# A two-layer hybrid decoder trunk: weight splits, first norm, softmax blocks, score rows and section order changed

## The chip, the cores and the metric

The kernel runs on one core of a Trainium2 chip. The metric is device time of one execution in microseconds (us), as the median of the runs. The profile is one execution, taken by the hardware profiler. The engines are named as the profile names them: PE is TensorE's matmul and PEld its weight load, DVE is VectorE, ACT is ScalarE, POOL is GpSimd, SP is the engine that issues most of the DMAs. L143 is line 143 of the kernel before.

## The reference

A trunk of two layers over 512 tokens of width 1024, all in fp32. One layer is:

```
h = rms_norm(x, norm_mix); proj = h @ w_in                   # 1024 -> 2832 columns, three head groups
y_a = gated_delta_net(...)   # 4 heads of 64: causal conv of width 4, silu, l2-norm of q and k,
                             # triangular solves, a recurrent state, rms_norm, silu gate
y_b = mlstm(...)             # 4 heads of 64: exponential input gate, sigmoid forget gate, stabilised
y_c = sliding_window(...)    # 8 query heads, 2 key heads, window 128, sink logits, rotary on 16 of 64
x = x + concat(y_a, y_b, y_c) @ w_out
x = x + square(relu(rms_norm(x, norm_mlp) @ w_up)) @ w_down  # 1024 -> 4096 -> 1024
x = x + sigmoid(rms_norm(x, norm_ple) @ w_ple_gate) * (p @ w_ple_proj)
```

After the second layer there is a last `rms_norm`. The attention's softmax takes, for each query and head, the scores of the window and one sink logit: it subtracts the largest, exponentiates, and divides by the sum with the sink's term. The rotary angles are position times eight frequencies.

## The kernel before, in words

**Layout.** Activations lie feature-major: 8 tiles `X` of 128 features x 512 tokens. A projection's output tile of 128 columns is a sum of 8 products over the input tiles.

**Three products for each.** To keep fp32 accuracy at the rate of a reduced format, each operand is split into a rounded high part and the rest (`whi`, `wlo` for weights, `xsh`, `xsl` for activations), and `mm3` (L165 to L167) multiplies high x high, high x low and low x high into one PSUM tile. Almost all TensorE time is in these three lines.

**The weight stream.** Feature-major weights come as 404 chunks of four 128 x 128 tiles (`w_load_`, from L137): a 256 KB DMA on the SP queue into one of two `raw` buffers, a cast on ScalarE to `whi` (L141), and a subtraction to `wlo` (L143). For the first `WPOOL` = 272 tiles of a layer, which is 68 chunks, the subtraction runs on GpSimd, after that on VectorE. Two chunks are asked for ahead of use.

**The start.** The token-major projections (`tok`, L271 to L273) need 8 input tiles, loaded and split (L190, L191), and 8 chunks of weights, split on VectorE (L264). Meanwhile `Norm.add` squares the input tiles on ScalarE (L204) and sums them on GpSimd and VectorE (L205). `Norm.finish` then sums over features with matmuls against ones (L212), takes a reciprocal root in small VectorE steps on 128 x 4 (`rsqrt`, L172 to L181), and spreads it over the partitions with a matmul against the identity (`rb`, L220). All norms work so.

**The mixing part of a layer** is a list of sections, opened by `seg(name)`: gates and their cumulative sums (`gates`, `rows`, `cols`), six projections with the convolution (`conv`: L440 scales, L443 is the first of four taps, L445 the others, on a tile that starts with three zeroed columns, L439), the squared lengths of queries and keys (`pss`, L455, with 32 output rows a tile, turned by transposes at L461), the triangular systems and their inverses (`decay`, `binv`, `dbl`), the scan over blocks, the mLSTM (`mlproj`, `ml`: scores `psq`, L729 and L730), the rotary tables and products (`rope`), the attention (`swa`), the output gates (`og`) and the output projection in two groups (`out1`, `out2`). The second score product, L730, multiplies 64 rows of the key tile with the low part of the queries, `mql`; two heads share an `mql` tile. The tiles `mqh`, `mql` and the attention's outputs `ych`, `ycl` come from one tag of eight buffers (`yq`).

**The attention** works by units of one head pair and one block of 128 queries, with four units pending: scores to PSUM, a copy of the previous block (L823), a masked copy of the own block (L826), the maximum (L828), its combination with the sink (L830, L831), the exponentials with their sums (L834), the sink's term (L837, L838), the division (L839 to L841), two transposes, two masks (L852, L855) and the products with the values.

**What sets the order.** Each engine works its instructions in a fixed order. It is made when the kernel is built, by a planner that simulates the engines and takes, of the instructions that are ready, the one with the highest priority. The priority is the place in the program, shifted by `tc.high_priority(offset)`. Weight loads and a few others are shifted by `HPRI` = 200; each section of each layer by its entry in the table `PRI`. So the table moves whole sections against the stream of projections on all engines at once.

**The end.** The last three row tiles are worked by halves of 256 tokens; for each half the norm is formed and the eight tiles are multiplied by it (L1039) and written out (L1040). The first half's products run on GpSimd, the second's on VectorE but for two.

## Time and profile before

| | |
|---|---|
| median of 3 runs | 1397.26 us (1394.84 to 1398.58) |
| span of the profiled execution | 1397.6 us |
| the profiled execution's own time beside the span | the span itself is used; nothing is added around it |
| PE busy | 1352.9 us |
| DVE, ACT, POOL busy | 839.1, 599.4, 325.1 us |
| DMA, mean over the span | 93 GB/s |

The span runs from the first to the last instruction. A line of a group reads: line, engine, operation, tile written <- tiles read, size, count | busy us, mean ns of one | idle time of the engine before them and what ended it. A line of the waits reads: engine and what waited, <- what it waited for: us in total, times, longest. In a timeline a line starts with its start in us and its duration. PE's times are modelled: a matmul's duration is longer than the distance to the next one, since they are pipelined, so distances from start to start are used where the pace counts.

### The profile page before, as it was taken

The numbers are of one execution on the slowest core, as the hardware profiler recorded it, in microseconds if no ns is written. First come the engines' busy times: TensorE is split into PE (matmuls) and PEld (weight loads), VectorE is DVE, ScalarE is ACT, GpSimd is POOL, SyncE is SP. The second block draws the span as 40 slices with busy tenths as digits, with TensorE's granted clock in tenths as the row PEclk, the third lists the DMA queues.
The fourth block names the chain that finished last, engine by engine and source line by source line (L and its number), as shares of the span: only waits on it lengthen the run. The fifth ranks groups of instructions, "written<-read, shape, count | busy, mean of one in ns | idle before, by whom it ended". The sixth has DMA issues, their size and how long they took to land.

```text
span 1397.6 us, 20344 instructions
## 1 busy us (share of the span) xinstructions
PE 1352.9 (97%) x7334; PEld 1113.3 (80%) x7334; DVE 839.1 (60%) x1749; ACT 599.4 (43%) x1236; POOL 325.1 (23%) x302
## 2 busy tenths in 40 slices
PE   7999899999999999999999899999999999999996
PEld 7667788778888888888896678887888888888886
DVE  6877978674344444454758688886544434444555
ACT  5374354254243242443535545634433324234443
POOL 4443632362000000010235455326400000000112
PEclk9999989999999999999999999999999999999998
DMA  4333222233333333332433322212333333233332
GB/s 152 99 99 89 55 57 77 69 98 98 98 99 95 95 97 98 99 98 91 142 106 99 108 69 63 78 54 91 99 98 98 97 99 95 95 98 98 98 98 76
DMA packets 88596, 130.04 MB, mean 93 GB/s; under 512 B 21408, under 2 KB 30112, under 8 KB 88496
## 3 DMA queue, kind: packets, MB, share of 16 engines
q1 hardware_dynamic: 87408, 127.71, 30.0%
q8 instruction: 57, 0.93, 0.3%
q10 hardware_dynamic: 1088, 1.05, 0.2%
q14 instruction: 43, 0.35, 0.1%
HBM read 123.18 MB, written 5.54 MB: 92 GB/s over the span
## 4 chain that ended last, share of the span: by engine, by line
PE 80%; DVE 9%; ACT 3%; issue 3%; POOL 2%; DMA 1%; SPq 0%; DVEq 0%; POOLq 0%; ACTq 0%
PE down L166 8%; PE down L165 8%; PE down L167 8%; PE up L167 8%; PE up L165 8%; PE up L166 8%; PE proj L165 2%; PE proj L167 2%; PE proj L166 2%; PE gate L165 2%; PE gate L167 2%; PE gate L166 2%; PE outp L166 2%; PE outp L165 2%; PE outp L167 2%
## 5 line engine op out<-in xcount | busy, mean ns | idle before, releaser
L141 ACT ACTIVATE whi<-raw 128x512 fp32r<-128x512 f32 x404 | 253.3, 630 | 530.5 <-PE down L166 201.3
L143 DVE TENSOR_TENSOR wlo<-raw,whi 128x512 fp32r<-128x512 f32 x268 | 187.1, 700 | 132.9 <-ACT whi L141 132.6
L143 POOL TENSOR_TENSOR wlo<-raw,whi 128x512 fp32r<-128x512 f32 x136 | 185.2, 1364 | 203.8 <-ACT whi L141 191.9
L205 POOL TENSOR_TENSOR acc<-acc,sq 128x512 f32<-128x512 f32 x34 | 49.0, 1440 | 700.4 <-ACT sq L204 700.0
L167 PE MATMUL up<-xsh,wlo 128*128 128x512 f32 x512 | 199.4, 390 | 1.2 <-POOL wlo L143 1.2
L165 PE MATMUL up<-xsh,whi 128*128 128x512 f32 x512 | 199.6, 390 | 0.0
L166 PE MATMUL up<-xsl,whi 128*128 128x512 f32 x512 | 199.2, 389 | 0.0
L165 PE MATMUL down<-hidh,whi 128*128 128x512 f32 x512 | 199.2, 389 | 0.0
L166 PE MATMUL down<-hidl,whi 128*128 128x512 f32 x512 | 197.9, 389 | 0.0
L167 PE MATMUL down<-hidh,wlo 128*128 128x512 f32 x512 | 197.9, 389 | 0.0
L165 PE MATMUL proj<-xsh,whi 128*128 128x512 f32 x304 | 125.2, 412 | 9.0 <-DVE rdst L781 4.5
L167 PE MATMUL proj<-xsh,wlo 128*128 128x512 f32 x304 | 124.6, 410 | 5.3 <-POOL wlo L143 5.3
L166 PE MATMUL proj<-xsl,whi 128*128 128x512 f32 x304 | 123.4, 406 | 0.0
L167 PEld LDWEIGHTS up<-xsh,wlo 128*128 128x128 f32 x512 | 96.1, 188 | 22.7 <-POOL wlo L143 2.8
L165 PEld LDWEIGHTS down<-hidh,whi 128*128 128x128 f32 x512 | 96.1, 188 | 20.0
L167 PEld LDWEIGHTS down<-hidh,wlo 128*128 128x128 f32 x512 | 96.1, 188 | 20.0
L965 DVE TENSOR_TENSOR X<-X,down 128x512 f32<-128x512 f32 x64 | 44.0, 688 | 113.3 <-PE down L167 113.3
L165 PEld LDWEIGHTS up<-xsh,whi 128*128 128x128 f32 x512 | 96.1, 188 | 19.8
L166 PEld LDWEIGHTS down<-hidl,whi 128*128 128x128 f32 x512 | 96.1, 188 | 19.8
L166 PEld LDWEIGHTS up<-xsl,whi 128*128 128x128 f32 x512 | 96.1, 188 | 19.8
L956 DVE SCALAR_TENSOR_TENSOR ha<-up,R 128x512 f32<-128x512 f32 x64 | 44.1, 691 | 100.3 <-PE up L167 89.8
L165 PEld LDWEIGHTS proj<-xsh,whi 128*128 128x128 f32 x304 | 59.5, 196 | 25.2 <-DVE mql L689 4.3
(359 smaller groups left out, 2306.5 us busy)
## 6 DMA issues: line engine op xcount, KB each, us to landing
raw<-wfm SPq DMA_DIRECT2D x404, 256.0 KB, 2.6
X<-xT SPq DMA_DIRECT2D x16, 256.0 KB, 4.5
raw<-wtm SPq DMA_DIRECT2D x16, 200.0 KB, 2.4
gr<-scr SPq DMA_DIRECT2D x8, 256.0 KB, 4.4
Mr<-scr SPq DMA_DIRECT2D x8, 256.0 KB, 3.5
xd<-X SPq DMA_DIRECT2D x8, 256.0 KB, 2.0
X<-xd SPq DMA_DIRECT2D x8, 256.0 KB, 2.9
praw<-pT SPq DMA_DIRECT2D x2, 512.0 KB, 3.7
```

What stands on the lines that cost most here:

```text
L141: A.activation(out=hi, in_=raw, func=ACTF.Copy)
L143: (G if (i % NCH) * WC < WPOOL else V).tensor_tensor(lo, raw, f(hi), ALU.subtract)
L165: PE.matmul(out=ps, lhsT=wh, rhs=ah, start=start and k == 0, stop=False)
L166: PE.matmul(out=ps, lhsT=wh, rhs=al, start=False, stop=False)
L167: PE.matmul(out=ps, lhsT=wl, rhs=ah, start=False, stop=stop and k == n - 1)
L205: (G if self.n < 6 else V).tensor_tensor(self.acc, self.acc, q, ALU.add)
L956: V.scalar_tensor_tensor(a_t, ps, 0.0, R, ALU.max, ALU.mult)
L965: V.tensor_tensor(X[m], X[m], ps, ALU.add)
```

## The change

- `WPOOL` is 0: all weight splits of the stream run on VectorE. `HPRI` is 250.
- The first norm takes its sums of squares from a second copy of the input, token-major (`xK`, four loads of 512 KB), by ScalarE with an accumulated sum (`token_sums`). The sums on GpSimd and the matmuls against ones are not needed there.
- The rotary angles are computed by token on 128 x 4 x 8 elements (`rope_tables2`), spread into two tiles and turned by 8 transposes; this stands after the first norm, not ahead of the rotary products.
- The norm's row is spread by a transpose of a broadcast column (`row_of`), not by a matmul against the identity.
- The sums of squares of queries and keys are formed token-major, with the squares as weights and two columns of indicators: no copy and no transposes afterwards.
- The first tap of the convolution runs on ScalarE and is the one without a shift, so that no zeroed columns are needed.
- The mLSTM's low queries get a tile for each head, with the other half zeroed, and the second score product uses all 128 rows.
- The softmax works on two blocks at a time, with three such pairs pending.
- Copies in the inverses and two of the output gates' products go from VectorE to ScalarE; the DeltaNet's norm gain is applied later, with the factor 0.5.
- Small tiles are padded to multiples of 64 bytes (`pad`).
- One matmul of zeros is issued at the start.
- At the end, only the group of two tiles of the second half stays on GpSimd; all other products run on VectorE.
- The table of section priorities is a new one.

```diff
 PRI = {
-    ("tok", 0): -400, ("vb", 0): 100, ("scan", 0): 60, ("og", 0): -400, ("out1", 0): -400, ("ya", 0): 100,
-    ("gates", 1): -50, ("cols", 1): 100, ("binv", 1): -200, ("dbl", 1): -50, ("mlproj", 1): 200, ("ml", 1):
-    30, ("rope", 1): 60, ("og", 1): -200, ("out1", 1): -200, ("ya", 1): 30, ("out2", 1): 100,
+    ("tok", 0): -400, ("vb", 0): -100, ("scan", 0): -600, ("og", 0): 30, ("out1", 0): -400, ("ya", 0): -600,
+    ("nrmk", 0): -600, ("ml", 0): -100, ("conv", 0): 150, ("decay", 0): 30, ("mlproj", 0): -300,
+    ("out2", 0): -100, ("dbl", 0): 30, ("ycb", 0): -600, ("cols", 0): 150, ("gates", 0): -50, ("binv", 0): -300,
+    ("gates", 1): -300, ("cols", 1): -100, ("binv", 1): 100, ("dbl", 1): 600, ("mlproj", 1): 30, ("ml", 1): 30,
+    ("rope", 1): 200, ("og", 1): -100, ("out1", 1): -100, ("ya", 1): 400, ("out2", 1): 200, ("ycb", 1): -50,
+    ("mlfin", 1): 60, ("rows", 1): -600, ("tok", 1): 30, ("decay", 1): 30, ("swa", 1): -50,
 }
-WPOOL = 272
-HPRI = 200
+PEND2 = 3
+WPOOL = 0
+HPRI = 250
...
+def pad(pool, shape, tag, name, bufs, dt=F32):
+    n = int(np.prod(shape[1:]))
+    if n % 16 == 0:
+        return pool.tile(shape, dt, tag=tag, name=name, bufs=bufs)
+    t = pool.tile([shape[0], -(-n // 16) * 16], dt, tag=tag, name=name, bufs=bufs)[:, 0:n]
...
+    with tc.high_priority(offset=4000):
+        zt = tp.tile([128, T], F32, tag="acc", name="zt", bufs=1)
+        G.memset(zt, 0.0)
+        pw = ps_tile([128, T], "pw")
+        for _ in range(1):
+            PE.matmul(out=pw, lhsT=zt[:, 0:128], rhs=zt, start=True, stop=True)
...
+    def token_sums(raw):
+        ss = pad(tp, [128, NB], "sst", "sst", 1)
+        for b in range(NB):
+            x_b = raw([128, D], "xk")
+            nc.sync.dma_start(out=x_b, in_=xK[b])
+            A.activation(out=x_b, in_=x_b, func=ACTF.Square, accum_out=ss[:, b:b + 1])
+        return ss
+    def row_of(ps, v):
+        PE.transpose(ps, v.broadcast_to([128, 128]), ident)
...
+    def rope_tables2(us, small):
+        pi = small([128, NB], "pi").bitcast(I32)
+        nc.sync.dma_start(out=pi, in_=pos)
...
+        for j in range(2):
+            src = us([128, NB, 128], "rsrc")
+            G.memset(src, 1.0 - j)
+            src4 = src.rearrange("p b (h e f) -> p b h e f", h=2, f=8)
+            for h in range(2):
+                for e in range(2):
+                    V.tensor_scalar(src4[:, :, h, e, :], k[:, j], -1.0 if j and not e else 1.0, None, ALU.mult)
+            pt = mm_tile("prt")
+            for b in range(NB):
+                PE.transpose(pt[:, b * 128:(b + 1) * 128], src[:, b, :], ident)
+            tab = us([128, T], "rtab")
+            A.activation(out=tab, in_=pt, func=ACTF.Copy)
+            nc.sync.dma_start(out=rope_d[j], in_=tab)
...
-            raw = us([128, 3 + T], "craw")
-            G.memset(raw[:, 0:3], 0.0)
-            V.tensor_tensor(raw[:, 3:3 + T], ps, R, ALU.mult)
+            raw = us([128, T], "craw")
+            V.tensor_tensor(raw, ps, R, ALU.mult)
...
-            V.tensor_scalar(c_t, raw[:, 0:T], s_l[:, w0:w0 + 1], None, ALU.mult)
+            A.activation(out=c_t, in_=raw, func=ACTF.Copy, scale=s_l[:, w0 + 3:w0 + 4])
...
-                PE.matmul(out=pss[32 * i:32 * i + 32], lhsT=ind, rhs=sq, start=True, stop=True)
+                for b in range(NB):
+                    PE.matmul(out=pss[:, b, i, :], lhsT=sq[:, b * 128:(b + 1) * 128], rhs=ind[:, 0:2], start=True,
+                              stop=True)
...
+                        q_l = yq("mql")
+                        mql.append(q_l)
+                        G.memset(f(q_l[halves[1 - e]]), 0.0)
...
-                PE.matmul(out=psq[:, 128 * J:T], lhsT=mkS[h][hs, js], rhs=mql[h // 2][hs, 128 * J:T], start=False, stop=True)
+                hs = slice(0, 128)
+                PE.matmul(out=psq[:, 128 * J:T], lhsT=mkS[h][hs, js], rhs=mql[h][hs, 128 * J:T], start=False, stop=True)
...
-            mx = tt([128, 2], "smx", bufs=2)
+            mx = tt([128, 2, 2], "smx", bufs=2)
             V.tensor_reduce(mx, rr, AX.X, ALU.max)
-            V.tensor_tensor(nm, mx, s8v[:, i], ALU.max)
-            V.tensor_scalar(nm, nm, -0.125, None, ALU.mult)
+            nsk_b = nsk[:, i].unsqueeze(1).broadcast_to([128, 2, 2])
+            V.scalar_tensor_tensor(nm, mx, -0.125, nsk_b, ALU.mult, ALU.min)
...
-                        e, r_ = (G, Rs) if g == 2 or not ts.start else (V, pr)
+                        e, r_ = (G, Rs) if (g == 2 and ts.start) else (V, pr)
```

More of the change, by code (lines that the diff above doesn't have):

```diff
@@ L275, in trunk @@
     XS = [None] * 8
-    nrm = Norm()
+    nrm = None
     for l in range(depth):
@@ L319, in trunk @@
             tok_mm(pst, k, *tok_weights(l, k))
+        with hp_():
+            rT, rI, R = (nrm or Norm(False)).finish(pa_tile, None if nrm else token_sums(ws))
         if l == 0:
-            for m in range(8):
-                nrm.add(m)
-        with hp_():
-            rT, rI, R = nrm.finish(pa_tile)
+            rope_tables2(us, tt)
         dump(f"R{l}", R)
@@ L417, in trunk, with proj @@
         fm_state = {"y": {}}
-        def proj():
-            ps = mm_tile("proj")
+        pj = [0]
+        def proj(alt=False):
+            pj[0] += 1
+            ps = (pa_tile([128, 512], "proj") if alt and pj[0] % 2 else mm_tile("proj"))
             mm3(ps, XS, True, True)
```

182 lines of the change are left out of this document (107 added, 75 removed).

## The prediction

> **What bounds the kernel now.** I read the page first (engine totals, then the row of the granted clock), then a table of busy time by stretches, then the waits of TensorE.
>
> ```profile
> span 1397.6 us, 20344 instructions
> PE 1352.9 (97%) x7334; PEld 1113.3 (80%) x7334; DVE 839.1 (60%) x1749; ACT 599.4 (43%) x1236; POOL 325.1 (23%) x302
> PEclk9999989999999999999999999999999999999998
> ```
>
> The profiled execution spans 1397.6 us and the median of the runs shown is 1397.26, so a sum made against the span can stand for the median unchanged. PE is busy for 1352.9 us: all its idle time is 44.7 us. A change to this kernel can win in three ways only: fewer or cheaper TensorE instructions, less of that idle time, or a better granted clock. The next view says where the last two lie. Its columns are the stretch, PE busy, PEld, DVE, ACT, POOL (with counts), granted clock, DMA share and GB/s.
>
> ```profile
> 0.00:300.00 300.00, 277.19 (x1820) 223.26 (x1821) 233.94 (x577) 146.87 (x369) 132.23 (x128) 0.96 0.29 87
> 350.00:650.00 300.00, 300.00 (x1326) 248.39 (x1325) 135.08 (x201) 110.13 (x176) 6.51 (x5) 1.00 0.32 97
> 700.00:1000.00 300.00, 291.52 (x1943) 236.34 (x1942) 228.39 (x573) 145.75 (x369) 137.63 (x128) 0.98 0.28 84
> ```
>
> The middle row is a layer's MLP: no idle, full clock, nothing to gain. The first and third are the mixing stages of the two layers: 22.8 and 8.5 us of idle, and a clock of 0.96 and 0.98. A matmul stage that loses 4% and 2% of its clock over 300 us loses up to 12 + 6 = 18 us, if TensorE had work throughout. Almost every edit lies in these stages or at the two ends. What ended TensorE's idle time:
>
> ```profile
> PE proj L167 <- POOL wlo L143: 5.3, 4, 2.4
> PE rb L1029 <- DVE rT L181: 4.8, 1, 4.8
> PE proj L165 <- DVE rdst L781: 4.5, 2, 2.9
> PE tok L272 <- DVE wlo L264: 3.7, 2, 2.2
> PE proj L165 <- DVE mql L689: 3.4, 2, 2.6
> PE pss L455 <- ACT sqq L454: 2.4, 1, 2.4
> PE up L167 <- POOL wlo L143: 1.2, 2, 0.6
> ```
>
> So the waits are for the low half of a weight made on GpSimd, and for VectorE results. There is no single wait to remove.
>
> **The change part by part.**
>
> *Equal-row scores.* The second mLSTM score matmul used 64 of the array's rows. One head of layer 0, in order of time (start, duration):
>
> ```profile
> 103.95 0.40 PE L167 MATMUL proj<-xsh,wlo 128*128 128x512 f32 x1
> 104.18 0.40 PE L729 MATMUL psq<-mqh,mkS 128*128 128x512 f32 x1
> 104.51 0.50 PE L730 MATMUL psq<-mql,mkS 64*128 64x512 f32 x1
> 104.94 0.44 PE L729 MATMUL psq<-mqh,mkS 128*128 128x384 f32 x1
> ...
> 106.81 0.50 PE L165 MATMUL proj<-xsh,whi 128*128 128x512 f32 x1
> ```
>
> A 512-column matmul among equals takes 0.23 us from start to start (103.95 to 104.18). The eight of this head take 106.81 - 104.18 = 2.63 us. At the equal-row pace they are 2 x 0.23 x (1 + 3/4 + 1/2 + 1/4) = 1.15 us, so 1.48 us less, and 11.8 us over 8 heads. If only the 64-row matmul itself gets cheaper (0.43 to 0.23 at 512 columns, in proportion about 0.5 x 8 x 4 x 0.2), it is some 4 us. I take 11, since the row of 128 rows beside it also runs at 0.33 in place of 0.23. All of it is TensorE time in a stage where TensorE sets the end. The price is a zeroed half per tile on GpSimd, off the path, and two more tiles of the eight that share one tag (a rival below).
>
> *Key and query sums, the broadcast of the norm, the first norm.* The group of the sums (busy, mean ns), then three pieces of the chain that ended last:
>
> ```profile
> L455 PE MATMUL pss<-sqq,cst 128*32 128x512 f32 x16 | 7.6, 620 | 2.4 <-ACT sqq L454 2.4
> 654.65 0.79 PE ss L212 x8
> 663.09 0.89 PE rb L220 x8
> 779.29 0.67 PE psst L461 x4
> ```
>
> The sums become 64 instructions with two columns; they are shaped like the eight of L212, 0.10 us each, so 6.3 us. Gone are 7.6 us, and two groups of four transposes at 0.67: 7.6 + 1.3 - 6.3 = 2.6 us saved. The 2.4 us wait for the squares becomes several short ones with other matmuls between; I take 2 of it. Bounds of the whole: nothing to 5; I take 4.5. The row broadcast becomes four transposes (0.67) in place of eight matmuls (0.89): 0.22 us in each of six norms, 1.3 us. The first norm loses its 8 sums (0.8) and the rotary tables add 8 transposes (1.3). Together 1 us.
>
> *Weight splits off GpSimd.*
>
> ```profile
> L143 DVE TENSOR_TENSOR wlo<-raw,whi 128x512 fp32r<-128x512 f32 x268 | 187.1, 700 | 132.9 <-ACT whi L141 132.6
> L143 POOL TENSOR_TENSOR wlo<-raw,whi 128x512 fp32r<-128x512 f32 x136 | 185.2, 1364 | 203.8 <-ACT whi L141 191.9
> L445 DVE SCALAR_TENSOR_TENSOR cc<-craw,sm,cc 128x512 f32<-128x512 f32 x36 | 36.1, 1003 | 0.8
> SPq L137 <- POOL wlo L143: 357.6, 115, 19.7
> ```
>
> 136 splits, 68 a layer, go from 1364 ns to 700 ns, a weight arrives 0.66 us earlier, and the SP queue, which waits for the split before it can refill its buffer, gets on sooner. TensorE's waits for GpSimd were 5.3 + 1.2 = 6.5 us: halved 3.3, all gone 6.5; I take 5, as VectorE is not free of waits. VectorE takes 68 x 0.70 = 47.6 us a layer. It has 300 - 234 = 66 us free in the first stage, 72 in the second, so it fits even if nothing comes back. Something does: L445, with two SBUF inputs of 512 columns, averages 1003 ns where a split of the same size takes 700, 36 x 0.3 = 11 us in this group alone. What lengthens it is seen at the start:
>
> ```profile
> 11.82 2.08 DVE L264 TENSOR_TENSOR wlo<-raw,whi 128x400 fp32r<-128x400 f32 x1
> 12.19 4.55 POOL L205 TENSOR_TENSOR acc<-acc,sq 128x512 f32<-128x512 f32 x3
> 18.01 0.57 DVE L264 TENSOR_TENSOR wlo<-raw,whi 128x400 fp32r<-128x400 f32 x1
> 8.00:12.00 4.00, 4.00 (x20) 3.99 (x20) 3.10 (x4) 4.00 (x9) 3.62 (x3) 1.00 1.04 385
> ```
>
> A split of 0.57 us takes 2.08 beside GpSimd's sums of squares. The first norm by token takes these sums away: TensorE's 3.7 us behind L264 can go. Against it, 2 MB more are loaded; behind the first tiles they meet an idle queue, in front of them they cost 2 MB / 385 GB/s = 5.4 us. I take -3, bounds -3.7 and +5.4. The waits for rdst and mql, 7.9 us, stand behind VectorE work that these collisions lengthen: I take half, 4, bounds 0 and 7.9.
>
> [...]
>
> *Softmax by two blocks.*
>
> ```profile
> L828 DVE TENSOR_REDUCE smx<-srr 128x2 f32<-128x256 f32 x32 | 13.0, 411 | 0.2
> L826 DVE COPY_PREDICATED srr<-lem,psc 128x256 f32<-128x256 uint8 x32 | 13.8, 436 | 2.2 <-ACT srr L823 1.3 <-PE psc L820 0.8
> L852 DVE TENSOR_TENSOR spc<-ptv,cst 128x256 f32<-128x256 f32 x32 | 13.2, 414 | 2.0 <-PE ptv L850 1.7
> L831 DVE TENSOR_SCALAR snm<-snm 128x2 f32<-128x2 f32 x32 | 7.5, 238 | 0.2
> L830 DVE TENSOR_TENSOR snm<-smx,s 128x2 f32<-128x2 f32 x32 | 6.7, 214 | 0.4
> ```
>
> L831 goes and L830 halves, and three more small steps like it halve too: 7.5 + some 4 x 3 = 19 us of VectorE over both layers, less what the wider forms cost. None of this is on TensorE's path while other matmuls cover it: I cost it at nothing. Without that cover it is the last rival below. The rest that goes to ScalarE (a convolution product, copies of the inverses, gates) is likewise put at nothing: ScalarE is busy 147 of 300 us. The cost if it is not hidden is a later cast of the next weight behind it. The 64-byte tiles have no row; by the 214 to 238 ns of the small forms above I bound them at 0 and a few us of VectorE, and take 0.
>
> *Rotary tables* move from the end of the mLSTM to the first norm, with one small load and two table writes on the SP queue ahead of weight loads. A write that waits there for its table holds up the weights behind it; before, the longest such wait was
>
> ```profile
> SPq L251 <- DVE k L239: 3.1, 1, 3.1
> ```
>
> I take 0 and keep 3.1 for the range: the old place had the same wait, and it goes.
>
> *Warm-up matmul and the end.* The clock dips followed stalls; with about half the stall time gone I take a quarter of the 18 us, 4 (bounds 0 and 9). The warm-up I put at 0, under the first loads. The last norm:
>
> ```profile
> 1383.15 5.53 POOL L1039 TENSOR_TENSOR fin<-X,Rs 128x256 f32<-128x256 f32 x8 [18.75 <-ACT Rs L1032]
> 1385.34 0.65 DVE L173 TENSOR_SCALAR rT<-rnw 128x2 int32<-128x2 int32 x1
> 1388.73 0.16 DVE L179 TENSOR_TENSOR rnw<-rT 128x2 f32<-128x2 f32 x1
> ```
>
> While GpSimd multiplies the first half, five small steps take 0.65 in place of 0.16: 5 x 0.49 = 2.5 us, on the last chain. These products go to VectorE; if they stand in front of the chain they cost up to 3 us. I take -2.5, bounds -3 and +1.
>
> *The section order* moves everything, and no row prices it: between the 26 us of idle left in the mixing stages after the first load (31.3 less 5.2 us) and a loss of like size. I take 0 beyond the terms above.
>
> Sum: 11 + 4.5 + 1 + 5 + 3 + 4 + 4 + 2.5 = 35 us; 1397.6 - 35 = 1362.6, say **1362 us**. With each term at its poor bound it is some 1399, at its good one 1350.
>
> **The rivals.**
>
> *The order fills the holes as well.* All idle of the mixing stages goes (26 us, against 5 + 3 + 4 + 2 in the sum) and half of the clock loss (9 against 4): 17 us more, about 1345, and lower if the scores, sums and end take their good bounds. For it: no stage has VectorE full. Against: in layer 0 a long chain precedes the first attention work.
>
> *Only TensorE's own work shrinks.* Waits for GpSimd become waits for VectorE, in one queue with everything else: 11 + 2.5 + 1 + 2.5 = 17 us, 1380. For it: VectorE rises towards 275 of 300 us before anything comes back.
>
> [...]
>
> *The change doesn't do what it says:* the long VectorE forms are due to GpSimd's other work (132 us busy in the first stage, splits only part), and ScalarE's new work delays the casts by what the scores save: 1396.
>
> *Slower.* The scores now take all eight tiles of the tag that the attention's outputs need; before, two were free. The values of the first attention heads must then wait until the scores have read theirs. If the new order puts the mLSTM late, attention runs after the projections that hid it, at VectorE's pace: the five groups above make 54 us, with as many like them some 85, so about 33 a layer after the pairing, of which its own matmuls hide about half. 16 us a layer: 1397.6 - 17 + 32 = 1412. It decides from 8.5 us a layer on, where it eats the 17 us.
>
> **How the numbers follow.** Forecast 0.53, fuller order 0.18, TensorE's work only 0.13, no effect 0.06, slower 0.10. Runs here differ by 0.3% and so I count a change within 0.3% (4 us) as none. Faster: 0.53 + 0.18 + 0.13 = 0.84; same 0.06; slower 0.10. The range runs from 1336, which takes in the fuller order, to 1388, which takes in the poorer terms: about 0.2 lies outside.
>
> **What will show it.** Scores: the L730 group with 128 rows and 0.23 us from start to start. Splits: no POOL group of wlo, the convolution group near 700 ns, and VectorE at no more than 250 us in each 300 us of mixing. Start: the token matmuls without the wait for wlo. End: small steps of 0.16 us throughout. It is wrong if PE's idle time does not fall below 30 us, if the clock in the mixing stages stays at 0.96, or if TensorE waits for ych late in a layer.

## The result and the profile after

The median is 1384.88 us (1383.06 to 1392.83, 8 runs) against 1397.92 us for the kernel before in the same series (1394.84 to 1400.17, 8 runs): a ratio of 0.9916, 95% interval 0.9895 to 0.9936. The forecast was 1362 us. The change makes the kernel faster by 13 us of the 35 that were summed up.

First the page of the kernel after: the span, TensorE's and the other engines' busy time, and the granted clock in 40 slices.

```profile
span 1383.5 us, 20187 instructions
PE 1353.4 (98%) x7348; PEld 1126.2 (81%) x7348; DVE 824.5 (60%) x1751; ACT 614.6 (44%) x1245; POOL 136.3 (10%) x152
PEclk9999979999999999999999997999999999999998
```

GpSimd went from 325.1 to 136.3 us, and VectorE is no busier (824.5 after 839.1) although it took 136 splits more. TensorE is as busy as before, 1353.4 after 1352.9 us, in a span that is 14.1 us shorter. So its idle time fell by 14.6 us (44.7 to 30.1), and its own work did not get shorter on balance. The next two views, of before and of after, cut the span into the mixing part of layer 0 with the start, the MLP of layer 0, and the same two of layer 1 (columns as in the prediction's view of stretches; the clock is the number behind POOL's count).

```profile
0.00:292.00 292.00, 269.19 (x1786) 217.13 (x1787) 225.94 (x569) 141.66 (x361) 124.31 (x123) 0.96 0.30 88
292.00:705.00 413.00, 412.40 (x1833) 341.11 (x1832) 203.46 (x308) 163.34 (x264) 40.67 (x30) 1.00 0.32 100
705.00:968.00 263.00, 255.12 (x1777) 206.81 (x1776) 203.08 (x537) 127.41 (x338) 115.06 (x113) 0.97 0.28 83
968.00:1398.00 430.00, 416.20 (x1942) 348.23 (x1940) 206.65 (x338) 167.00 (x275) 45.09 (x38) 0.98 0.31 95
```

```profile
0.00:277.00 277.00, 266.17 (x1802) 223.28 (x1802) 206.23 (x549) 148.28 (x363) 48.24 (x65) 0.93 0.34 99
277.00:695.00 418.00, 415.85 (x1830) 341.16 (x1830) 210.51 (x327) 164.89 (x268) 20.84 (x16) 1.00 0.36 99
695.00:953.00 258.00, 254.05 (x1791) 215.65 (x1791) 196.72 (x517) 134.57 (x341) 47.70 (x58) 0.96 0.31 85
953.00:1384.00 431.00, 417.29 (x1928) 346.06 (x1926) 211.06 (x360) 166.82 (x276) 19.52 (x16) 0.99 0.33 95
```

The mixing parts gained 15 and 5 us, the MLPs lost 5 and 1. And the clock in the mixing is lower than before: 0.93 after 0.96, 0.96 after 0.97. This is not one execution's chance: over the eight runs of after the mean granted clock is 0.975 (0.969 to 0.979), and over the 25 runs of before beside e5 and e6 below it is 0.983 (0.976 to 0.988).

**The account used below.** Three numbers add up to the span: idle is the span less PE busy; clock loss is the span times one less the mean granted clock (0.982 before, 0.975 after); work is the rest, an estimate of what TensorE would need at full clock.

| | span | idle | clock loss | work |
|---|---|---|---|---|
| before | 1397.6 | 44.7 | 25.2 | 1327.7 |
| after | 1383.5 | 30.1 | 34.6 | 1318.8 |
| difference | -14.1 | -14.6 | +9.4 | -8.9 |

The clock loss is an upper bound: at half clock small products do not take twice as long (e9 below: 32 ns became 53), and what they do not lose is missing in the work. It also moves from one execution to the next: two kernels with the same order in the first mixing part, after and e3, show 34.6 and 41.5 us, before and e4 25.2 and 22.4.

**What the single edits show in the trace of after.** The scores, one head, TensorE in order of time:

```profile
101.09 0.39 PE L808 MATMUL psq<-mqh,mkS 128*128 128x512 f32 x1
101.32 0.39 PE L810 MATMUL psq<-mql,mkS 128*128 128x512 f32 x1
101.55 0.34 PE L808 MATMUL psq<-mqh,mkS 128*128 128x384 f32 x1
...
102.14 0.40 PE L191 MATMUL proj<-xsh,whi 128*128 128x512 f32 x1
```

A 512-column product now takes 0.23 us from start to start in both lines, and the first six together 1.05 us. Then the group of the splits and that of the convolution's taps (busy, mean ns):

```profile
L169 DVE TENSOR_TENSOR wlo<-raw,whi 128x512 fp32r<-128x512 f32 x404 | 292.3, 725 | 179.4 <-ACT whi L167 178.6
```

```profile
L524 DVE SCALAR_TENSOR_TENSOR cc<-craw,sm,cc 128x511 f32<-128x511 f32 (+2 forms) x36 | 27.5, 763 | 5.0 <-ACT cc L522 4.5
```

All 404 splits are on VectorE at 725 ns, and the taps take 763 ns on average after 1003. Their median hardly moved (750 after 752): what went are single taps of up to 1835 ns; the longest now takes 1110. What TensorE still waits for, the longest first:

```profile
PE ss L1113 <- ACT sq L1104: 2.3, 1, 2.3
PE rb L231 <- DVE rT L207: 2.1, 1, 2.1
PE up L192 <- DVE xsl L217: 2.1, 4, 0.7
```

In the whole list there is no wait for rdst, mql or a split of GpSimd, and the last norm's is 2.1 us after 4.8, with small steps of 0.16 us throughout (1374.71 us and after).

### The profile page after: what moved, and what is told of

The parts are those of the page before. It is cut to its first block, busy times and chain, and to the rows that moved or that the text cites. A ratio compares the mean times of both kernels' runs of the same rounds, so it can differ in the third digit from the quotient of the medians.

```text
span 1383.5 us, 20187 instructions
## 1 busy us (share of the span) xinstructions
PE 1353.4 (98%) x7348; PEld 1126.2 (81%) x7348; DVE 824.5 (60%) x1751; ACT 614.6 (44%) x1245; POOL 136.3 (10%) x152
## 3 DMA queue, kind: packets, MB, share of 16 engines
q10 hardware_dynamic: 1088, 1.05, 0.2%
## 4 chain that ended last, share of the span: by engine, by line
PE 84%; DVE 9%; ACT 2%; DMA 2%; issue 2%; SPq 0%; DVEq 0%; ACTq 0%
PE down L191 9%; PE down L193 9%; PE down L192 8%; PE up L191 8%; PE up L192 8%; PE up L193 8%; PE proj L191 3%; PE proj L192 3%; PE proj L193 3%; PE gate L191 2%; PE gate L193 2%; PE gate L192 2%; DVE wlo L169 2%; PE outp L192 2%; PE outp L191 2%
## 5 line engine op out<-in xcount | busy, mean ns | idle before, releaser
L169 DVE TENSOR_TENSOR wlo<-raw,whi 128x512 fp32r<-128x512 f32 x404 | 292.3, 725 | 179.4 <-ACT whi L167 178.6
L244 POOL TENSOR_TENSOR acc<-acc,sq 128x512 f32<-128x512 f32 x29 | 39.7, 1369 | 862.5 <-ACT sq L243 857.0
L214 DVE TENSOR_TENSOR hidl<-hf,hidh 128x512 fp32r<-128x512 f32 x64 | 44.2, 691 | 42.9 <-ACT hidh L213 42.9
```

The source lines that it names most:

```text
L169: (G if (i % NCH) * WC < WPOOL else V).tensor_tensor(lo, raw, f(hi), ALU.subtract)
L214: V.tensor_tensor(lo, src, f(hi), ALU.subtract)
L244: (G if self.n < 6 else V).tensor_tensor(self.acc, self.acc, q, ALU.add)
```

## The experiments

Times and ratios against the kernel before, run on the same chip; the account is from one profile each. Where a section, a size or an instruction is changed, the planner makes a new order for all engines, so each run has a plan of its own.

| | median us | ratio (95%) | idle | clock loss | work |
|---|---|---|---|---|---|
| after | 1384.88 | 0.9916 (0.9895 to 0.9936) | 30.1 | 34.6 | 1318.8 |
| e1 edits, old order | 1390.71 | 0.9940 (0.9917 to 0.9963) | 36.7 | 25.0 | 1324.8 |
| e2 new order alone | 1437.34 | 1.0281 (1.0261 to 1.0302) | 54.5 | 72.0 | 1313.9 |
| e3 after, MLP tiles moved | 1383.06 | 0.9880 (0.9862 to 0.9897) | 28.7 | 41.5 | 1313.6 |
| e4 before, MLP tiles moved | 1401.92 | 1.0028 (1.0016 to 1.0041) | 42.9 | 22.4 | 1334.5 |
| e5 splits back on GpSimd | 1408.77 | 1.0065 (1.0045 to 1.0084) | 42.5 | 40.7 | 1318.8 |
| e6 splits moved, alone | 1417.11 | 1.0141 (1.0112 to 1.0170) | 47.9 | 43.9 | 1324.0 |
| e7 scores as before | 1389.10 | 0.9937 (0.9914 to 0.9960) | 25.9 | 30.5 | 1329.8 |
| e8 products added | 1405.95 | 1.0051 (1.0030 to 1.0073) | 32.3 | 33.7 | 1340.1 |
| e11 sums as before | 1395.57 | 0.9992 (0.9977 to 1.0006) | 40.9 | 36.2 | 1316.6 |
| e12 order by layer, MLP tiles moved | 1380.34 | 0.9884 (0.9861 to 0.9907) | 34.0 | 23.4 | 1320.1 |
| e14 e12, one priority changed | 1381.27 | 0.9885 (0.9868 to 0.9902) | 30.4 | 33.1 | 1317.2 |
| e15 e12, four priorities changed | 1377.06 | 0.9845 (0.9823 to 0.9867) | 30.8 | 26.2 | 1321.9 |

### The order: e1 and e2

e1 is the kernel after with the table of priorities and the `HPRI` of before, e2 the kernel before with those of after.

```diff
-PRI = { ... the table of after ... }
-HPRI = 250
+PRI = { ... the table of before ... }
+HPRI = 200
```

> All edits of the change with the old priority table and the old shift of 200 for weights. Theory A (the new order thins out the projections under the attention, and the clock drops there): the time at half clock falls back from about 58 us to some 38, and the kernel comes out at 1376 to 1382, faster than the changed kernel. Rival B (the edits themselves gain less than was summed, the order is what gained): 1388 to 1396. The mean granted clock of the run tells them apart: 0.982 under A, 0.975 under B.

> The kernel before with the new priority table and the shift of 250 only. Theory A: the clock falls (0.975) without anything gained: 1400 to 1415. Rival B: the order alone gives a good part of the 13 us: 1385 to 1393.

e1 came out between the two theories: the clock of A (0.982 in the profile) with the time of B. e2 lost far more than A said, at a clock of 0.950. Without the new order the edits bring 0.60% in place of 0.84%: the order is worth 3 us by the ratios and the profiles, 6 by the medians, and since the two intervals overlap this gain is not settled. Alone the order loses 2.8%: it pays at best together with the edits. What goes with it in the clock is seen in the first 270 us of before, e1 and e12 (the old order in layer 0), then of after and e2 (the new one); one window from each kernel:

```profile
0.00:270.00 270.00, 247.96 (x1694) 200.38 (x1695) 210.96 (x546) 131.57 (x343) 113.69 (x116) 0.96 0.29 87
```

```profile
0.00:270.00 270.00, 257.04 (x1781) 212.95 (x1782) 198.79 (x541) 143.54 (x355) 46.18 (x64) 0.98 0.33 101
```

```profile
0.00:270.00 270.00, 253.84 (x1778) 210.96 (x1779) 197.98 (x541) 143.34 (x355) 46.64 (x64) 0.98 0.34 100
```

```profile
0.00:270.00 270.00, 259.40 (x1773) 218.11 (x1774) 200.10 (x540) 143.74 (x355) 48.09 (x64) 0.93 0.34 98
```

```profile
0.00:270.00 270.00, 247.53 (x1650) 201.84 (x1651) 203.26 (x546) 130.34 (x339) 105.84 (x111) 0.90 0.28 82
```

In these kernels the old order has 0.96 to 0.98 (e4: 0.96) and the new one 0.90 to 0.93 (e3: 0.92), with the edits and without them. The other runs widen both ranges. With the new table e5, e7, e8 and e11 have 0.94; e9 and e13, whose edits lie behind this part, have 0.93 and 0.95, so one order alone moves by 0.02 or so. With the old table e6, which moves only the splits, has 0.91. So the new table goes with a lower clock in this part, but an edit that makes the planner order anew can lower it as much under the old one. Against e1 the new order has 6.6 us less idle and 6.0 less work, for 9.6 more clock loss. What stands ahead of the dips is told under the clock below.

### The MLP: e3 and e4

The eight additions behind the down products of the first group tell TensorE's pace there, since each comes when 24 products are done. First of before, then of after, the second and the last of the eight:

```profile
353.45 0.69 DVE L965 TENSOR_TENSOR X<-X,down 128x512 f32<-128x512 f32 x1 [1.05 <-PE down L167]
...
386.09 0.69 DVE L965 TENSOR_TENSOR X<-X,down 128x512 f32<-128x512 f32 x1 [1.59 <-PE down L167]
```

```profile
340.90 0.69 DVE L1056 TENSOR_TENSOR X<-X,down 128x512 f32<-128x512 f32 x1 [1.08 <-PE down L193]
...
373.86 0.69 DVE L1056 TENSOR_TENSOR X<-X,down 128x512 f32<-128x512 f32 x1 [1.62 <-PE down L193]
```

32.64 us for six times 24 products before, 226.7 ns each; 32.96 after, 228.9 ns each. No instruction there was changed. Over the 64 tiles of the two layers that is 64 x 0.053 = 3.4 us. What did change is where the tiles lie: with the smaller mixing tiles all tiles that follow moved. By the addresses of the built kernels the hidden high parts (`hidh`, the moving operand) lie 256 bytes from the weight parts (`whi`, the stationary one) modulo 2048 before, and 576 after. e3 puts 1472 unused bytes ahead of the MLP's tiles of after, which makes it 0; e4 puts 320 ahead of those of before, which makes it 576.

```diff
+        hp.tile([128, 368], F32, name="shift")     # e3, in after; e4: 80 elements, in before
```

> The changed kernel with 1472 unused bytes per partition in front of the MLP's tiles, so that the hidden tiles lie at the same place modulo 2 KB as the weight tiles; nothing else moves. Theory M (the down products' pace of 229.0 ns in place of 226.7 comes from where the hidden tiles lie): the pace goes back to 226.7 ns, 8 x 192 x 2.3 = 3.5 us, and the gate's with it, some 4 us in all: 1380 to 1382. Rival N (it comes from VectorE or DMA traffic): 229 ns stays, 1385.

> The kernel before with 320 unused bytes per partition in front of the MLP's tiles, so that hidden and weight tiles stand to each other as in the changed kernel. Theory M: the down products slow from 226.7 to 229.0 ns and the kernel takes 3.5 to 4.5 us more, 1401 to 1403. Rival N: no change, 1397 to 1399.

The same two additions in e3, and then in e4:

```profile
342.08 0.69 DVE L1057 TENSOR_TENSOR X<-X,down 128x512 f32<-128x512 f32 x1 [1.05 <-PE down L193]
...
374.73 0.69 DVE L1057 TENSOR_TENSOR X<-X,down 128x512 f32<-128x512 f32 x1 [1.59 <-PE down L193]
```

```profile
351.70 0.69 DVE L966 TENSOR_TENSOR X<-X,down 128x512 f32<-128x512 f32 x1 [1.08 <-PE down L167]
...
384.66 0.69 DVE L966 TENSOR_TENSOR X<-X,down 128x512 f32<-128x512 f32 x1 [1.62 <-PE down L167]
```

32.65 us in e3, 32.96 in e4: the pace follows the placement in both directions, and e4 is slower than before by 0.28%. Of the down products only those with `hidh` slowed: from start to start they take 231.6 ns with `whi` and 229.2 with `wlo` in after and in e4, and 226 to 227 in before and e3; those with `hidl`, the low parts, take 226 in all four. Since `hidl` and `wlo` lie to each other modulo 2048 as `hidh` and `whi` do, that distance alone does not tell which products slow, and why these addresses cost a product 2 to 5 ns is not settled here. That e3 is faster than after is not settled by the times either, whose intervals overlap; in its profile the clock took back what the MLP gained.

### The splits: e5 and e6

e5 is after with `WPOOL` = 272, e6 is before with `WPOOL` = 0.

> The changed kernel with the first 68 splits of each layer back on GpSimd. Theory P (the prediction's term: splits on GpSimd cost waits of TensorE and lengthen VectorE's two-input forms): 6 to 12 us slower than the changed kernel, 1390 to 1397, the convolution's taps back above 900 ns and TensorE's waits for wlo from GpSimd back at 4 us or more. Rival Q (other engines' waits take their place and VectorE's load is what counts): within 3 us of 1385.

> The kernel before with all weight splits on VectorE and nothing else. Theory P: 5 to 9 us faster than before, 1389 to 1393. Rival Q: within 3 us of 1398, or slower.

With everything else of the change the move is worth 1.5% (the ratios 1.0065 and 0.9916), some 21 us, four times the term of the prediction and more than either theory said: 12.4 us of idle and 6.1 of clock loss come back in e5's profile. Its waits for GpSimd's splits are 3.8 us of that; more came from other waits. The taps follow the splits in both directions: their mean is 926 ns in e5 and 792 in e6, after 763 in after and 1003 in before. Alone the move costs 1.4%, where the theory behind the prediction's term had it gain. In e6 TensorE waits for VectorE at the convolution:

```profile
PE proj L165 <- DVE craw L440: 8.1, 3, 5.2
```

and the clock loss rises by 18.7 us. So the same move pays beside the rest of the change and costs without it. Whether it is the work taken off VectorE or the order that decides, these two runs do not tell.

### The scores and the sums: e7 and e11

e7 is after with the second score product over 64 rows and one `mql` tile for two heads; e11 is after with the sums of squares of queries and keys as before.

```diff
-                PE.matmul(out=psq[:, 128 * J:T], lhsT=mkS[h][hs, js], rhs=mql[h][hs, 128 * J:T], start=False, stop=True)
+                PE.matmul(out=psq[:, 128 * J:T], lhsT=mkS[h][hs, js], rhs=mql[h // 2][hs, 128 * J:T], start=False, stop=True)
```

> The changed kernel with the 64-row second score product and shared low tiles. The term of the sum was 11 us; the traces give 19.1 us of psq pace before and 11.5 after, some 7.6, and about 1.5 more in the product that follows each. Theory R (that is TensorE time on the path): 1391 to 1396. Rival S (it is given back to waits and the clock): 1383 to 1388.

The work is 11.0 us more than in after, which is the term of the prediction, in part by luck: from start to start the products of the scores take 20.3 us in e7 and 11.5 in after, 8.7 less, and with the expectation's 1.5 for the products behind them it is some 10. The time is only 3 to 4 us longer (by the ratios, by the medians), between the two forecasts and with intervals that overlap: this plan has 4.2 us less idle and 4.1 less clock loss.

```diff
-                for b in range(NB):
-                    PE.matmul(out=pss[:, b, i, :], lhsT=sq[:, b * 128:(b + 1) * 128], rhs=ind[:, 0:2], start=True, stop=True)
+                PE.matmul(out=pss[32 * i:32 * i + 32], lhsT=ind, rhs=sq, start=True, stop=True)
...
+        ssr = us([128, T], "ssr")
+        A.activation(out=ssr, in_=pss, func=ACTF.Copy)
+        pst_ = ps_tile([128, NB, 4, 32], "psst")
+        for b in range(NB):
+            PE.transpose(pst_[:, b].rearrange("p g c -> p (g c)"), ssr[:, b * 128:(b + 1) * 128], ident)
```

> The kernel after with the key/query sums of squares as before the change: sixteen 128x512 products into 32 rows, ScalarE's copy and four transposes in each layer's place, in place of the 64 products of two columns. Theory H (two-column products cost 7.1 us of TensorE against 6.3 and drop the clock at 62 to 69 us, for 3.4 us more; the wait for the copy was covered or short): 1380 to 1384. Theory of the prediction (this edit saves 4.5 us): 1388 to 1391.

That expectation, that the edit is worth nothing or less, fell: e11 is 10.7 us slower than after. It is not TensorE's work, which is 2.2 us less in e11. In after's chain of work that ended last the two-column products of layer 1 stand with 0.115 us each, not 0.10, and in layer 0 the last few fall into half clock, at 0.21:

```profile
739.76 2.77 PE pss L536 x24
```

From start to start all 64 take 7.6 us in after; the 16 wide products of e11 take 5.9 and its transposes 0.9. What e11 loses is 10.8 us of idle, and the two longest of its waits are for a cast of weights on ScalarE and for the convolution's scaled tile on VectorE:

```profile
PE proj L191 <- ACT whi L167: 6.6, 2, 5.2
PE proj L191 <- DVE craw L519: 4.7, 1, 4.7
```

In after the first of these is 1.1 us and the second is not there. In e11's timeline that cast comes at 81.29 us, and between it and the one before stand eight exponentials and one step of the convolution in ScalarE's order. The two casts:

```profile
77.92 0.61 ACT L167 ACTIVATE whi<-raw 128x512 fp32r<-128x512 f32 x1
...
81.29 0.61 ACT L167 ACTIVATE whi<-raw 128x512 fp32r<-128x512 f32 x1
```

So most of the edit's worth here lies in two waits of the plan, one in each layer. That the copy itself is what pushed the cast and the scaled tile back was not shown.

### The clock: e8, e9, e10, e13

In after the clock is half for 3.4, 6.8 or 17.1 us at a time, always a multiple of 3.41 us in the trace's record of the clock (the end apart): eight times in the mixing parts, 58 us in all, after nine times and 38 us in before. What stands in the 3.41 us ahead of such a stretch is of two kinds. The first line is ahead of the stretch of before that starts at 173.20 us, the second ahead of that of after at 168.10, the third a region of after a little later:

```profile
169.79:173.20 3.41, 0.89 (x4) 0.79 (x5) 3.41 (x6) 0.28 (x1) 3.41 (x4) 1.00 0.00 0
...
164.69:168.10 3.41, 3.41 (x121) 3.41 (x120) 2.23 (x5) 0.96 (x2) 0.00 (x0) 0.99 0.33 87
170.00:180.00 10.00, 10.00 (x158) 9.87 (x157) 5.58 (x15) 6.54 (x24) 0.31 (x1) 0.67 0.01 2
```

Ahead of the first TensorE is idle for 2.5 of 3.4 us; ahead of the second it is never idle. Sorted in this way, five of the nine stretches of before follow 1.2 to 2.5 us of idle time (20 us at half clock) and four follow none (17 us). In after two follow 1.5 and 2.1 us of idle (10 us) and six follow 0.3 or less (48 us). So the dips behind stalls did halve, as the prediction had it, and those that follow no stall nearly trebled. What runs ahead of these six are the 32x32 products of the inverses (t1p and y1p, most of the 121 and 158 instructions above), and once the two-column sums. e2's large loss is mostly of the other kind: eight of its ten stretches, 106 of 133 us, follow 1.2 us of idle or more. For the second kind the profile's idle time explains nothing, since these products run without a gap (3.41 of 3.41 us busy ahead of the stretch at 168.10).

e8 adds 192 products of 128 columns, which nothing reads, under the attention.

```diff
+            for _ in range(6):
+                PE.matmul(out=pt[:, 384:512], lhsT=skh[0][:, 0:128], rhs=sqS[i][0][:, bs], start=True, stop=True)
```

> The changed kernel with six added 128-column products in each of the 32 attention value steps, written to unused columns and read by nothing: 192 products, at least 192 x 0.056 = 11 us of TensorE work at full clock. Theory C (the clock falls to half in the attention since its small products leave the array idle in each window): the half-clock time of the mixing stages falls from 58 us to below 30, and up to half of the 11 us comes back: 1388 to 1392. Rival D (the clock goes by something else): the half-clock time stays and the full price or more is paid: 1396 or more.

The clock loss stays (33.7 after 34.6), the mixing parts still have 58 us at half clock, and the work rises by 21.3 us: a product takes 0.11 us from start to start, twice the estimate of 0.056, a quarter of the 226 ns that a down product of 512 columns takes. But in both layers the half-clock stretches of e8's mixing part end ahead of the added products, which stand from 188.6 to 234.1 us and from 876.8 to 932.2. So the run shows the price of filling; whether denser work inside a dip lifts the clock it does not test.

e9 adds small products where the clock is 1.00 otherwise, in the MLP.

```diff
+                if m == 4 and g in (1, 2):
+                    n = ((32, 64), (128, 32))[l][g - 1]
+                    fl = mm_tile("fil")
+                    for k in range(128):
+                        PE.matmul(out=fl[0:n, 0:32], lhsT=ident[0:n, 0:n], rhs=X[3][0:n, 0:32], start=True, stop=True)
+                        if l == 1 and g == 2 and k % 4 == 3:
+                            PE.matmul(out=fl, lhsT=hid[0][0][:, 0:128], rhs=hid[0][0], start=True, stop=True)
```

> The kernel after, with products added that nothing reads, at four places in the middle of the down products of the MLP (second and third group of each layer), where the granted clock of the kernel after is 1.00. Place 1: 128 fp32 products of a 32x32 tile by 32 columns. Place 2: the same with 64x64. Place 3: the same with 128x128. Place 4: 32x32 again, but with a 128x128 product of 512 columns after every fourth. Theory H (the clock follows how much of the 128x128 array is at work: columns streamed times the share of rows and columns in use; below some 0.30 of what it could do in a stretch of 3.4 us it goes to half, and comes back after a stretch above some 0.40): half clock at places 1 and 2, for 3.4 to 10 us each, and 1.00 at places 3 and 4; whole time 1425 to 1445, most of it the price of the added products. Theory R (the clock follows the columns streamed or the pauses between products, whatever the tile's rows): places 1, 2 and 3 alike, since the columns are the same. Theory N (the low clock in the mixing comes from something else in the section, such as the load of the other engines): 1.00 at all four places.

One run, 1514.78 us. In windows, a stretch near the start of place 1 and a later one, then a later one of places 2, 3 and 4:

```profile
445.00:448.00 3.00, 3.00 (x101) 3.00 (x98) 0.69 (x1) 0.38 (x1) 0.00 (x0) 1.00 0.44 122
449.00:455.00 6.00, 6.00 (x116) 6.00 (x115) 0.00 (x0) 0.00 (x0) 0.00 (x0) 0.50 0.01 3
...
556.00:566.00 10.00, 10.00 (x96) 10.00 (x96) 0.00 (x0) 0.00 (x0) 0.00 (x0) 0.50 0.01 2
...
1160.00:1200.00 40.00, 40.00 (x190) 40.00 (x189) 0.00 (x0) 0.00 (x0) 0.00 (x0) 0.50 0.00 0
...
1303.00:1335.00 32.00, 32.00 (x227) 19.47 (x225) 0.00 (x0) 0.00 (x0) 0.00 (x0) 0.50 0.00 1
```

And the added products by themselves while the clock is still full, at places 1, 2 and 3, then at place 1 at half clock (count, shortest, median and longest in ns, first and last start):

```profile
L1058 PE MATMUL fil<-X,cst x101: 190/191/192, 444.8 to 448.0; 32*32 32x32 f32 x101
...
L1058 PE MATMUL fil<-X,cst x88: 219/219/240, 544.9 to 550.0; 64*64 64x32 f32 x88
...
L1058 PE MATMUL fil<-X,cst x24: 191/276/276, 1155.5 to 1157.9; 128*128 128x32 f32 x24
...
L1058 PE MATMUL fil<-X,cst x116: 236/236/237, 448.8 to 454.9; 32*32 32x32 f32 x116
```

From first to last start that is 32, 59 and 104 ns an instruction, and 53 at half clock. Half clock at all four places, where two were expected to hold. So products do drop the clock, in a section where little else is going on, and while TensorE is without a gap in the profile: the theory that the low clock comes from other engines' load falls. At places 3 and 4 the added products ran slower than estimated, which by the theory is why these dropped too: with a 128x128 tile one instruction took 104 ns for its 32 columns, and a round of four 32x32 products and a 512-column one takes 0.79 us.

e13 adds 64 products at each of the same places, with two or four times the columns.

```diff
+                    r, c, n = (((128, 128, 64), (64, 64, 128)), ((64, 128, 128), (128, 32, 128)))[l][g - 1]
+                    for _ in range(64):
+                        PE.matmul(out=fl[0:c, 0:n], lhsT=ident[0:r, 0:c], rhs=X[3][0:r, 0:n], start=True, stop=True)
```

> The kernel after, with 64 fp32 products (128 instructions) added that nothing reads, at four places in the middle of the down products (second and third group of each layer). In e9 the pace of 128x128 fp32 products of 32 columns was set by the loading of their tile (101 ns each), and that of small tiles was not. Place 1: tile of 128 rows by 128 columns, 64 columns streamed (by 101 ns, 0.53 of the array's time is at work). Place 2: 64x64, 128 columns streamed (all of the time, a quarter of the array: 0.25). Place 3: 64 rows by 128, 128 streamed (0.50). Place 4: 128 rows by 32, 128 streamed (0.25). Theory H (activity is the columns streamed times the share of rows and columns in use, lost under some 0.30 and back over some 0.40): half clock in places 2 and 4, 1.00 in places 1 and 3. Rival R (the columns streamed alone): 0.53, 1.0, 1.0 and 1.0, so no half clock anywhere. Rival S (small tiles or mixed shapes as such): half clock in 2, 3 and 4. Time 1435 to 1465, the price of the added products.

One run, 1441.06 us. The four places:

```profile
441.00:455.00 14.00, 14.00 (x129) 14.00 (x127) 0.69 (x1) 0.63 (x1) 0.00 (x0) 1.00 0.13 38
543.00:557.00 14.00, 14.00 (x129) 13.83 (x128) 0.69 (x1) 0.51 (x1) 0.00 (x0) 1.00 0.11 35
1147.00:1160.00 13.00, 13.00 (x119) 13.00 (x118) 0.69 (x1) 0.00 (x0) 0.00 (x0) 1.00 0.08 23
1249.00:1262.00 13.00, 13.00 (x121) 13.00 (x120) 0.69 (x1) 0.20 (x1) 0.00 (x0) 1.00 0.09 28
```

No drop at all. The theory that rows times columns in use count, as written down, falls: 64x64 tiles with 128 columns hold the clock at a quarter of the array (1.00 in the second line). Its thresholds, 0.30 and 0.40, were the author's estimate, and no run shows them. The rival that only the columns count fits this run, but not e9. As an estimate worked out from both: 128 fp32 columns take 0.11 us here (128 instructions in 14 us), 0.86 ns a column, so the share of time in which columns stream is 0.86 in e9's place 1 (32 columns each 32 ns), 0.47 in its place 2 (59 ns) and 0.26 in its place 3 (104 ns), and 0.5 and three times 1.0 in e13. Place 1 of e9 dropped at 0.86 with 32x32 tiles; place 1 of e13 held at 0.5 with whole ones. The columns alone do not decide, nor, by a margin as thin as the estimate, does the product with the array's share (0.25 held in e13, 0.26 with a whole array dropped in e9). Something between would fit the two runs: by the same estimate, with the square root of the product as the weight, places 1 to 3 of e9 lie at 0.21 to 0.27, its place 4 at 0.36 (0.23 us of whole array and 0.06 of the rest in 0.79), and all of e13 at 0.5 and above. This is fitted to the runs that it describes, and no run has tested it: what the clock follows stays open.

e10 puts a product of 128 columns after every fourth of the 32x32 ones of the inverses.

```diff
+                if u % 4 == 3:
+                    PE.matmul(out=fl, lhsT=At[0][:, 0, :], rhs=Yd[:, 0:4, :].rearrange("p u c -> p (u c)"), start=True, stop=True)
```

> The kernel after, with a 128x128 product of 128 columns added (read by nothing) after every fourth of the 32x32 products of the two stages t1p and y1p: 64 in all, by estimate 0.21 us each, 13.7 us. The kernel after has 58 us at half clock in the two mixing sections, some 24 us of them in and right behind these stages (168 to 182 and 844 to 861 us). Theory H: most of these 24 us go (58 down to 30 to 42), which pays back 8 to 14 us, and the time is 1382 to 1391. Rival (the clock does not follow the array's activity, or the drops move elsewhere): half clock stays at 50 us or more and the full price shows, 1395 to 1402.

Both expectations missed: the median is 1532.5 us, a ratio of 1.0964 (1.0942 to 1.0985), with 108.7 us of clock loss and 110.0 of idle. The planner brought the whole stage forward, away from the projections; TensorE then stands idle for 27.4 us and streams little afterwards (two windows):

```profile
110.00:120.00 10.00, 0.00 (x0) 0.00 (x0) 9.11 (x27) 0.00 (x0) 0.00 (x0) 0.50 0.00 0
130.00:140.00 10.00, 10.00 (x80) 7.76 (x80) 0.00 (x0) 0.00 (x0) 0.00 (x0) 0.50 0.01 2
```

As a test of whether denser work saves the clock the run says nothing. It shows how long the low state can last where little else is there: 99 us on end, of which TensorE is busy for 59.

### A faster order: e12, e14, e15

e12 is after with the old order in layer 0, the new one in layer 1, and e3's filler; `HPRI` stays at 250.

> The kernel after with the section order of before in layer 0 and the new one in layer 1, and 1472 bytes of filler ahead of the MLP's tiles so that the hidden parts stand to the weight parts as before (modulo 2048 bytes). From e1's first mixing section (276.3 us, against 277.4), after's second (258.0) and the 3.5 us of the MLP that the filler gave back in e3's trace: 1376 to 1381, with some 34 us at half clock in the mixing (13.7 of e1's first and 20.5 of after's second). Rival (an order is fitted to the whole plan, and halves of two do not add up): 1383 or above.

1380.34 us, as expected. In its profile the clock loss is 11.2 us less than in after, and idle 3.9 more. The intervals of the two ratios overlap, so that it is faster than after is likely but not settled.

e14 and e15 change one and four priorities of e12, picked by the rule of e9 as it then stood, applied to the order of the products:

```diff
-("rope", 1): 200, ("decay", 1): 30
+("rows", 0): -300, ("ml", 0): 30, ("rope", 1): -300, ("decay", 1): 150      # e15; e14: rows alone
```

The sections `rows` and `ml` of layer 0 have no entry in e12's table, so they went from 0 to -300 and 30, and not from -600 and -100 as the expectations say.

> e12 with one priority changed (rows of layer 0: -600 to -300), picked because theory H, applied to the order in which the products then stand on TensorE, gives 43 us at half clock where it gives 60 for e12's order (38 measured there in the mixing) and 61 for that of after (58 measured). Theory H: 15 to 33 us at half clock in the mixing, time 1370 to 1379. Rival (the order's other waits decide, or the rule does not foresee the clock): 1380 or above, half clock 35 or more.

> e12 with four priorities changed (layer 0: rows -600 to -300, ml -100 to 30; layer 1: rope 200 to -300, decay 30 to 150), picked in the same way: theory H gives 28 us at half clock for this order of the products, against 60 for e12's. Theory H: 5 to 25 us at half clock in the mixing, time 1364 to 1377, if the idle time of TensorE stays at e12's. Rival (other waits decide): 1380 or above.

In the mixing parts the record of the clock has 58 us at half in e14 and 41 in e15: neither forecast of the theory holds, e14 came out as the rival said, and the rule did not foresee the clock of a new order. e15 is nevertheless the fastest kernel of the study, 1377.06 us, below after with intervals that do not touch. In its profile, which is of its longest run (span 1378.9 us, clock 0.981), the idle is that of after and the clock loss 8.4 us less; over its four runs the mean clock is 0.984, after 0.975 in after.

## Why the prediction was wrong

The direction and the range (1336 to 1388) held; the size was off by 21 us by the two profiles that the account uses, 22 by the medians. In the account above the prediction's 35 us were 14.5 of work (scores 11, sums 2.5 of their 4.5, the broadcasts 1), 16.5 of waits (splits 5, start 3, rdst and mql 4, the end 2.5, 2 of the sums) and 4 of clock. Measured were 8.9, 14.6 and -9.4: short by 5.6, 1.9 and 13.4.

**The clock: the step that failed.** "The clock dips followed stalls; with about half the stall time gone I take a quarter of the 18 us." This took all dips for one kind. Those behind stalls did halve, from 20 to 10 us at half clock in the mixing parts, which at half speed is worth at most 5 us, near the 4 of the sum. The others, behind small products without a stall, were there in before with 17 us and grew to 48; the sum had no term for them, and the bounds, 0 to 9, left out a loss. e9 shows that such products drop the clock without a gap (0.50 at four places, TensorE busy for 6.00 of 6.00 us at the first). e1 against after and before against e2 show a lower clock with the new order (in e2 mostly behind stalls), e6 that another plan can have it under the old one. That it is the new order's grouping of small products that made these dips grow is argued from what stands ahead of them, from e9 and from e13; no run that changed only the grouping has shown it. The 13.4 us are an upper bound, by what small products do not lose at half clock and by what the clock moves between executions.

**The MLP: "nothing to gain".** There was something to lose. The part that 64-byte tiles and smaller buffers played was put at 0 by their VectorE time; what they moved was the address of the MLP's tiles, and that cost 3.4 us by the pace of the down products, shown both ways by e3 and e4. By this estimate it is most of the 5.6 us that the work fell short by.

**The section order: 0 was nearly right, as a sum.** Its 3 to 6 us are what is left of 12.6 gained and 9.6 lost.

**The waits: right in sum, in part by luck, since the shares are others.** Idle of 30.1 us is just above the bound of 30 that was named. The splits, put at 5 within 3.3 to 6.5, are worth some 21 us in e5 (18.5 of it in the profile), the sums 11 in e11; each of these is a difference between two plans, so they do not add up to the change. The end went as worked out: the small steps take 0.16 us and the wait for them fell by 2.7.

**The scores: right, a little high.** 11 predicted, 11.0 of work in e7, some 10 when counted from start to start, at 0.23 us a product. In the time they bring 3 to 4 us; e7's plan has less idle and a better clock.

**The sums: wrong in their terms.** The prediction priced what goes by busy time and durations, 7.6 and 1.3 us, in which pipelined products overlap; from start to start it is 7.1 and 0.9 in before and 5.9 and 0.9 in e11. The two-column products take 7.6 us, not 6.3. So 2.6 us were to be saved, and next to e11 TensorE takes 0.9 more (2.2 by the account, which also holds what the two plans differ in); with the waits the edit still pays.

**VectorE beside GpSimd.** The taps take 763 ns on average after 1003, with GpSimd busy for 136.3 us after 325.1, and 926 in e5 with the splits back on GpSimd; whether GpSimd's work alone makes the difference was not shown. VectorE's 225 and 226 us in the two windows of 300 us (0 to 300, 700 to 1000) stay below the 250 that were named.

**The rivals.** The time is nearest to that of "only TensorE's own work shrinks" (1380), but for the opposite reason: the waits did go, and something else took the gain. The move of the splits alone does cost time (e6, 1.0141), but beside the rest of the change it pays (1.0065 in e5, 0.9916 in after). The slower case, attention run behind the projections that hid it, did not come: TensorE waits 0.6 us for an attention output (ycl) in all.

## What to carry to other kernels

Read the granted clock beside TensorE's busy time, stretch by stretch: a busy TensorE that streams few columns through small tiles can fall to half clock (0.50 in e9), and a gain in idle time can be lost there (14.6 us of idle gained here, up to 9.4 lost to the clock). Before a loss of clock is put down to stalls, look at what runs just ahead of each dip. A change of tile sizes moves the addresses of everything after it, so look at the pace of products that were not touched (226.7 ns became 228.9 here). Where a planner makes the order, price an edit with its plan: the move of the splits brought some 21 us in one plan and cost some 20 in another.

## What the hardware showed that was not expected

- The clock fell to half without any idle time in the profile: with 32x32, 64x64 and 128x128 fp32 products of 32 columns in the MLP (e9, 0.50); with 128x128 and twice, 64x64 and four times the columns it did not (e13, 1.00). It stayed there for 54.6 us at e9's third place.
- A round of 32x32 and 128x128 products took longer than its parts. In e9, TensorE in order of time:

```profile
1297.59 0.43 PE L1058 MATMUL fil<-X,cst 32*32 32x32 f32 x8
1297.95 0.49 PE L1060 MATMUL fil<-hidh 128*128 128x512 f32 x1
1298.38 0.43 PE L1058 MATMUL fil<-X,cst 32*32 32x32 f32 x8
```

  A round takes 0.79 us (1297.59 to 1298.38). Eight small instructions at 32 ns and one 512-column product at 0.23 us would be 0.49, so some 0.30 us of a round go with its two changes of shape, by this estimate. What takes that time was not shown.
- Down products of the same shape take 226.7 or 228.9 ns on average by where the MLP's tiles lie: a shift of these tiles by 1472 or 320 bytes changes it, in both directions (e3, e4).
